# Output weights with the latents' gates folded in, and a context tile with weights of its own

## The chip, the cores and the metric

The kernel runs on one core of a Trainium2 chip. A core has five engines that work side by side, each through its own queue of instructions in order: TensorE (PE, matrix products into PSUM), VectorE (DVE), ScalarE (ACT), GpSimd (POOL) and SyncE (SP), which here issues nearly all DMAs. The metric is the time of one execution in microseconds on the device. Before the change the median of three runs is 2587.82 us (2584.45 to 2589.98).

## The reference

One layer of a hybrid diffusion backbone is computed for 128 context tokens and 2048 latent tokens, all in fp32. Cut to the part that the change touches:

```python
def block(x, s0, mod, ...):
    sh1, sc1, ga1, sh2, sc2, ga2 = mod
    h = rmsnorm(x, norm_mix_l) * (1.0 + sc1) + sh1
    o, s_new = mixer(h, s0, ...)          # ends with: out @ w_out_l
    x = x + ga1 * o
    h = rmsnorm(x, norm_ffn_l) * (1.0 + sc2) + sh2
    x = x + ga2 * (jnp.square(jax.nn.relu(h @ w_ff1_l)) @ w_ff2_l)
    return x, s_new
```

The mixer runs a gated DeltaNet scan forwards and backwards in chunks (four heads of 128) beside a gated spatial MLP (four groups of 128), and projects both together by `w_out` (1024 x 1024). `ga1` is a row of 1024 gates, one for each output column. Context and latent tokens are conditioned by different vectors, so they have different gate rows, and the weights are the same for both. Since `ga1` scales columns of the output, `ga1 * (out @ w_out)` equals `out @ (w_out * ga1)`.

## The kernel before

Tokens are worked on in 17 tiles of 128: tile 0 is the context, tiles 1 to 16 are the latents. The program has a first stage (modulation vectors, input projection, convolution; about 0 to 455 us), a **first scan pass** over the tiles 0 to 16 (forward scan, units 0 to 16), a **second scan pass** (backward scan, units 17 to 33: tile 0, then tiles 16 down to 1), and an MLP stage from about 1235 us on. During the second pass each tile's output is normalised, multiplied by its gate of the mixer, projected by `w_out`, and added to the residual (`o_steps`, line 1317).

**Products in three parts.** Most large products are made by `mm3` (line 238): both operands are split into a high and a low part in fp32r, and three matmuls (high x high, high x low, low x high) are accumulated, at lines 242 to 244. `split_w` (line 194) makes the parts of a weight piece of 128 x 512: the high part by a ScalarE copy, the low part by a DVE subtraction; with a scale (lines 199 and 200) the rows are scaled at the same time. Some products are plain fp32 matmuls of one instruction: the scan's (`quad`, line 1011), the first modulation sums (line 353, two stationary columns) and the row scale of the first stage (line 482).

**The output projection.** `load_wo` (line 1305) loads the sixteen pieces of `w_out` (two column halves n, eight row pieces k) through the stage pool `sp`, which has NS = 4 buffers, and splits them with `wscale`, a scale for each row. It also loads the two halves of the latents' gate row, spread over 128 partitions (`wrow`, line 232). For each tile `trans` (line 1340) transposes the mixer's two halves on TensorE (line 1350) and splits the result into oH (ScalarE, line 1353) and oL (DVE, line 1354). `proj` (line 1359) accumulates two weight pieces a step, eight steps a tile. After the last piece of a half, DVE multiplies the PSUM result by the gate (line 1373, into tmp) and adds tmp to x (line 1374), which is stored to x2_d. Tile 0 loads the context's gate row for this (line 1371).

**What else the second pass does.** For tiles above 8 the steps of `h2_steps` (line 852) prepare the MLP's input in the same pass; their `put` (line 900) splits pieces into opH and opL in the stage buffers and stores them to hop_d. The scan's operands (KK, QK, gb, kt, kT, vt, qT) come back from device memory, and SP issues their loads.

**What sets the order.** Each step is an event with a time in units (`at`, line 1390; `spread`, line 1393): unit i's scan lies at i - 0.51 to i + 1.06 in the first pass, its weights at 16.75 to 18.2, tile 0's `trans` at 18.36 to 18.64 and its `proj` at 18.66 to 19.66. The steps are written in the order of their times, and the framework's planner (line 2015) then orders each queue by its own estimate of when operands and buffers are ready, in favour of what was written first. So a load can be issued far ahead of its use when its buffer is free. "Fill" steps are held behind the scan and its preparation on TensorE by added dependencies (line 1491). Each queue is then strictly in order: an instruction that waits holds all behind it.

Of the kernel before, what the change touches and what calls it, by code (L numbers as in the profile page):

```python
# [8 lines left out]
F32 = mybir.dt.float32  # L9
# [4 lines left out]
ALU = mybir.AluOpType  # L14
# [3 lines left out]
P = 128  # L18
D = 1024
KT = D // P  # L20
# [3 lines left out]
H = 4  # L24
# [41 lines left out]
def hybrid_step(  # L66
# [7 lines left out]
    V, A, G, T = nc.vector, nc.scalar, nc.gpsimd, nc.tensor  # L74
    load = nc.sync.dma_start
    store = nc.sync.dma_start
# [36 lines left out]
    hop_d = {(g, o): dp.tile([P, 4, 2, 4, P], F32, name=f"hop_{g}_{o}_d") for g in range(2) for o in range(1, 8)}  # L113
    z_d = [dp.tile([4 if a else 1, P, 2, NK, P], F32, name=f"z{a}_d") for a in range(5)]
    s1_d, s2_d = ([dp.tile([4, P, NK, P], F32, name=f"s{i}{g}_d") for g in range(2)] for i in (1, 2))
    t_d = {(i, k): dp.tile([P, 512], F32, name=f"t{i}_{k}_d") for i in (5, 6, 7, 4) for k in range(NK)}


# [70 lines left out]
    def raw_w(src, pool=None, tag="w"):  # L189
        t = (pool or wp).tile([P, 512], F32, tag=tag, name="raw")  # L190
        load(out=t, in_=src)
        return t
# [13 lines left out]
    def load_split(src, scale=None):  # L206
        return split_w(raw_w(src, sp, "raw"), scale)
# [24 lines left out]
    def wrow(row):  # L232

        t = w512("row")
        load(out=t, in_=row.to_broadcast([P, 512]))
        return t

    def mm3(ps, trip, first=True, last=True, more=False):

        n = len(trip)  # L240
        for i, (lh, ll, rh, rl) in enumerate(trip):
            T.matmul(ps, lh, rh, start=first and i == 0, stop=False, skip_group_check=more)  # L242
            T.matmul(ps, lh, rl, start=False, stop=False, skip_group_check=more)  # L243
            T.matmul(ps, ll, rh, start=False, stop=last and i == n - 1, skip_group_check=more)  # L244
# [51 lines left out]
    with ExitStack() as ph:  # L296
# [5 lines left out]
        def pj(dt=F32):  # L302
            return ppj.tile([P, 512], dt, tag="pj", name="pj", bufs=3)
# [657 lines left out]
    with ExitStack() as ph:  # L961
# [332 lines left out]
        def fpart(name):  # L1294
            return fp.tile([P, 512], F32, tag="part", name=name, bufs=5)
# [6 lines left out]

        ga1 = []

        def load_wo(n, k):
            if k == 0:
                ga1.append(wrow(mod_d[1:2, 2 * D + n * 512 : 2 * D + n * 512 + 512]))
                WO.append([])
            WO[n].append(load_split(w_out[0, k * P : (k + 1) * P, n * 512 : (n + 1) * 512], wscale[:, k : k + 1]))

        def o_loads(u):
            t = u["t"]
# [4 lines left out]
        def o_steps(du):  # L1317
            t = du["t"]
            out = []
            u = {}  # L1320

            def norm():
                du["ob"] = w512("ob")
                load(out=du["ob"], in_=ob_d[t * P : (t + 1) * P, :])
                o, ga = du["o"], du["ga"]
                ss = smp.tile([P, 4], F32, tag="oss", name="oss")
                junk = fp.tile([P, P], BF16, tag="junk", name="junk", bufs=1)
                for h in range(H):
                    A.activation(junk, o[:, h, :], AF.Square, accum_out=ss[:, h : h + 1])
                r2 = smp.tile([P, 4], F32, tag="r2", name="r2")  # L1330
                rr = smp.tile([P, 4], F32, tag="rr", name="rr")
                V.tensor_tensor(out=r2, in0=rq[:, t, :], in1=rq[:, t, :], op=ALU.mult)
                V.tensor_tensor(out=r2, in0=r2, in1=ss, op=ALU.mult)
                rsqrt_cols(rr, r2, 4, 1.0 / P, EPS)
                V.scalar_tensor_tensor(out=rr, in0=rr, scalar=0.5, in1=rq[:, t, :], op0=ALU.mult, op1=ALU.mult)
                for h in range(H):
                    V.scalar_tensor_tensor(out=o[:, h, :], in0=o[:, h, :], scalar=rr[:, h : h + 1],
                                           in1=ga[:, h * P : (h + 1) * P], op0=ALU.mult, op1=ALU.mult)

            def trans(half):  # L1340
                def f():
                    if half == 0:
                        u["H"], u["L"] = [], []
                        u["x"] = [w512("x"), w512("x")]
                        for n in range(2):
                            load(out=u["x"][n], in_=xrow(t)[:, n * 512 : (n + 1) * 512])
                    src = du["o"] if half == 0 else du["ob"].rearrange("p (h d) -> p h d", h=H)
                    ps = pj().rearrange("p (h d) -> p h d", h=H)
                    for h in range(H):
                        T.transpose(ps[:, h, :], src[:, h, :], ident)  # L1350
                    hs = hp.tile([P, 4, P], F32R, tag="h", name="oH")
                    ls = hp.tile([P, 4, P], F32R, tag="h", name="oL")
                    A.copy(hs, ps)
                    V.tensor_tensor(out=ls, in0=ps, in1=f32(hs), op=ALU.subtract)
                    u["H"] += [hs[:, i, :] for i in range(4)]
                    u["L"] += [ls[:, i, :] for i in range(4)]
                return f

            def proj(n, k0):
                def f():  # L1360
                    if k0 == 0:
                        u["ps"] = pj()
                    for k in (k0, k0 + 1):
                        mm3(u["ps"], [(u["H"][k], u["L"][k]) + WO[n][k]], first=k == 0,
                            last=k == KT - 1)
                    if k0 == KT - 2:
                        sl = slice(n * 512, (n + 1) * 512)
                        tmp = fp.tile([P, 512], F32, tag="ug" if n else "vg", name="tmp")
                        ga = ga1[n]
                        if cond(t) == 0:  # L1370
                            ga = wrow(mod_d[0:1, 2 * D + n * 512 : 2 * D + n * 512 + 512])
                        x = u["x"][n]
                        V.tensor_tensor(out=tmp, in0=u["ps"], in1=ga, op=ALU.mult)
                        V.tensor_tensor(out=x, in0=x, in1=tmp, op=ALU.add)
                        du["x2"] = u["x"]
                        store(out=x2_d[t * P : (t + 1) * P, sl], in_=x)
                return f

            for n in range(2):
                for k0 in range(0, KT, 2):  # L1380
                    out.append(proj(n, k0))
            return [norm, trans(0), trans(1)], out
# [10 lines left out]
        def spread(t0, t1, steps, kind):  # L1393
            for j, st in enumerate(steps):
                at(t0 + (t1 - t0) * (j + 0.5) / len(steps), st, kind)
# [84 lines left out]
        flat = flat[NF:]  # L1480
        spread(p2[4], p2[5], flat, "fill")
        wo = [lambda n=n, k=k: load_wo(n, k) for n in range(2) for k in range(KT)]
        spread(16.75, 17.4, wo[:6], None)
        spread(17.45, 18.2, wo[6:], None)
        tend = max(e[0] for e in events if e[3] == "prep")
# [574 lines left out]
```

## Time and profile before

| | before |
|---|---|
| median of three runs | 2587.82 us (2584.45 to 2589.98) |
| the profiled execution | 2589.03 us |
| its span, first to last instruction | 2587.1 us |
| granted TensorE clock | 0.999 |
| DMA, mean over the span | 221 GB/s |

In the tables of windows each engine has its busy time in that stretch and, in brackets, its number of instructions; after them stand the granted clock, the mean busy share of the 16 DMA engines and the GB/s moved. Matmuls are pipelined: their recorded durations overlap, so the distance between two starts is the cost of one in a row. In the view of one line the three figures are the shortest, the median and the longest duration in ns, then the first and the last start in us. In the chain of waits, which follows the work that ended last back to what released it, each piece has its start, its length and its name; the "by line" row gives each line's share of the stretch.

### The profile page before, as it was taken

Reading aid. Unit: us, or ns where it says so; the run is one execution under the profiler, and the core shown is the slowest. Engines: PE = TensorE matmul, PEld = TensorE weight load, DVE = VectorE, ACT = ScalarE, POOL = GpSimd, SP = SyncE. Lnnn points to the kernel's source line nnn. Section 1 sums busy time; section 2 is a strip of 40 time slices with the busy share of each in tenths; the row PEclk is TensorE's granted clock in tenths of the full one; section 3 lists DMA queues with packets and bytes.
Section 4 is the critical chain, followed back from the end, with each engine's and each line's share of the span. In section 5 each row is a group of like instructions: output and inputs, shape, how many; then the busy total and the mean of one; then the engine's idle time right before and its main releaser. Section 6 shows DMA issues by size and latency. Waiting matters only on the chain.

```text
span 2587.1 us, 44754 instructions
## 1 busy us (share of the span) xinstructions
PE 2547.4 (98%) x15556; PEld 2154.5 (83%) x15556; DVE 1805.3 (70%) x3738; ACT 1221.0 (47%) x3051; POOL 233.7 (9%) x448
## 2 busy tenths in 40 slices
PE   9999999999999999999999999999999999999998
PEld 5899998788888787788888888888888888888887
DVE  5867757766677878886678876666665557784875
ACT  4755556555555667764345543333342432342442
POOL 3112212111111111210000000000000000000000
PEclk9999999999999999999999999999999999999999
DMA  8977737644454656885868788444479979786683
GB/s 287 300 219 213 211 111 253 229 154 155 144 160 151 215 177 235 281 275 183 280 205 252 230 289 293 122 115 118 120 239 368 345 257 327 266 257 204 223 266 112
DMA packets 494695, 571.88 MB, mean 221 GB/s; under 512 B 35124, under 2 KB 297564, under 8 KB 490886
## 3 DMA queue, kind: packets, MB, share of 16 engines
q1 hardware_dynamic: 494470, 569.04, 67.8%
q8 instruction: 122, 2.00, 0.3%
q14 instruction: 103, 0.84, 0.1%
HBM read 389.23 MB, written 179.67 MB: 220 GB/s over the span
## 4 chain that ended last, share of the span: by engine, by line
PE 86%; DMA 6%; DVE 5%; ACT 2%; issue 1%; SPq 0%; POOL 0%; POOLq 0%; DVEq 0%; ACTq 0%
PE f L242 16%; PE f L244 16%; PE f L243 16%; PE pj L242 7%; PE pj L244 6%; PE pj L243 6%; PE pd L1011 4%; PE f L1646 2%; PE pm L242 1%; PE pm L244 1%; PE pm L243 1%; PE pt L626 1%; DMA QK<-qk_d 1%; DMA raw<-in_w_mod_dram 1%; DMA hop_d<-opL 1%
## 5 line engine op out<-in xcount | busy, mean ns | idle before, releaser
L242 PE MATMUL f<-hop,zH 128*128 128x512 f32 (+1 forms) x976 | 376.2, 386 | 1.2 <-ACT zH L1532 1.2
L243 PE MATMUL f<-hop,zH 128*128 128x512 f32 (+1 forms) x976 | 376.1, 386 | 0.0
L244 PE MATMUL f<-hop,zL 128*128 128x512 f32 (+1 forms) x976 | 376.1, 386 | 0.0
L242 PE MATMUL f<-hop,wH 128*128 128x512 f32 x896 | 355.2, 397 | 0.1
L243 PE MATMUL f<-hop,wH 128*128 128x512 f32 x896 | 349.0, 390 | 0.0
L244 PE MATMUL f<-hop,wL 128*128 128x512 f32 x896 | 347.9, 390 | 0.0
L1532 ACT CAST zH<-zraw 128x512 fp32r<-128x512 f32 x240 | 146.4, 620 | 284.6 <-DMA zraw<-s_d 86.9
L242 PEld LDWEIGHTS f<-hop,zH 128*128 128x128 f32 x976 | 183.3, 188 | 38.5 <-ACT zH L1532 1.6
L244 PEld LDWEIGHTS f<-hop,zL 128*128 128x128 f32 x976 | 183.3, 188 | 37.3 <-DVE zL L1526 0.4
L243 PEld LDWEIGHTS f<-hop,zH 128*128 128x128 f32 x976 | 183.3, 188 | 36.9 <-issue 0.2
L1526 DVE TENSOR_TENSOR zL<-zraw,zH 128x512 fp32r<-128x512 f32 x240 | 162.6, 687 | 72.2 <-ACT zH L1532 55.1
L244 PEld LDWEIGHTS f<-hop,wL 128*128 128x128 f32 x896 | 168.2, 188 | 35.3
L242 PEld LDWEIGHTS f<-hop,wH 128*128 128x128 f32 x896 | 168.5, 188 | 32.8 <-issue 0.5
L243 PEld LDWEIGHTS f<-hop,wH 128*128 128x128 f32 x896 | 168.5, 188 | 32.3
L242 PE MATMUL pj<-kH,wH 128*128 128x386 f32 (+2 forms) x568 | 190.5, 338 | 1.3 <-ACT junk L602 1.1
L243 PE MATMUL pj<-kL,wH 128*128 128x386 f32 (+2 forms) x568 | 189.5, 335 | 0.5 <-POOL kL L511 0.5
L244 PE MATMUL pj<-kH,wL 128*128 128x386 f32 (+2 forms) x568 | 189.7, 335 | 0.0
L185 POOL TENSOR_TENSOR r<-rsq,nhalf 128x1 f32<-128x1 f32 (+1 forms) x37 | 25.1, 679 | 1418.0 <-DVE rsq L184 1418.0
L572 DVE SCALAR_TENSOR_TENSOR cv<-pj,vec,cv 128x384 f32<-128x384 f32 (+2 forms) x164 | 87.0, 539 | 52.7 <-ACT cv L569 51.4
L242 PEld LDWEIGHTS pj<-kH,wH 128*128 128x128 f32 x568 | 107.0, 189 | 4.6 <-issue 2.6
L1532 ACT CAST wH<-s 128x512 fp32r<-128x512 f32 x96 | 59.4, 621 | 105.5 <-DVE s L1526 103.5
L243 PEld LDWEIGHTS pj<-kL,wH 128*128 128x128 f32 x568 | 107.4, 189 | 1.4 <-POOL kL L511 0.8
(410 smaller groups left out, 5703.9 us busy)
## 6 DMA issues: line engine op xcount, KB each, us to landing
zraw<-z_d SPq DMA_DIRECT2D x212, 256.0 KB
raw<-in_w_ff_dram SPq DMA_DIRECT2D x128, 256.0 KB
hop<-hop_d SPq DMA_DIRECT2D x28, 1024.0 KB
z_d<-c SPq DMA_DIRECT2D x96, 256.0 KB
zraw<-s_d SPq DMA_DIRECT2D x96, 256.0 KB
raw<-in_w_mod_dram SPq DMA_DIRECT2D x80, 256.0 KB
r<-in_w_ff_dram SPq DMA_DIRECT2D x80, 256.0 KB
s_d<-s SPq DMA_DIRECT2D x64, 256.0 KB
```

The source lines that it names most:

```text
L185: G.tensor_tensor(out=out, in0=t[:np_, :n], in1=nhalf[:np_, :n], op=ALU.pow)
L242: T.matmul(ps, lh, rh, start=first and i == 0, stop=False, skip_group_check=more)
L243: T.matmul(ps, lh, rl, start=False, stop=False, skip_group_check=more)
L244: T.matmul(ps, ll, rh, start=False, stop=last and i == n - 1, skip_group_check=more)
L572: V.scalar_tensor_tensor(out=cv[:, o : o + m], in0=ps[:, s + sh : s + sh + m], scalar=convw[:, w, j : j + 1], in1=cv[:, o : o + m], op0=AL ...
L626: T.matmul(ps[:, i * P : (i + 1) * P], kTt[:, i * P : (i + 1) * P], rhs[:, i * P : (i + 1) * P], start=True, stop=True)
L1011: T.matmul(p[:, h, :], lhs[:, h, :], rhs[:, h, :], start=True, stop=True)
L1526: V.tensor_tensor(out=out, in0=a, in1=b, op=op)
L1532: A.copy(h, src)
L1646: T.matmul(ps[:, c : c + P], self.raw[m, kh][:, kp, :], x0[kh][:, kp, :], start=first and kp == 0, stop=last and kp == 3)
```

## The change

In the first pass, between the event times 2.0 and 15.0, `gate_wo` loads each of the sixteen pieces of `w_out`, multiplies it on DVE by the latents' gate row, and stores it to a new array wo_d in device memory. `load_wo` then loads the pieces from there. So the projection of tiles 1 to 16 already holds the gate: line 1373's multiplication goes for them, and x is added to straight from PSUM. Tile 0 needs other gates, so it takes `w_out` itself, piece by piece through the stage buffers and without a split: its transposed activations are scaled by `wscale` on DVE into one fp32 tile, and each piece is one fp32 matmul in place of `mm3`'s three. It keeps the multiplication by its own gate row.

```diff
+    wo_d = {(n, k): dp.tile([P, 512], F32, name=f"wo{n}_{k}_d") for n in range(2) for k in range(KT)}
...
+        def wo_piece(n, k):
+            return w_out[0, k * P : (k + 1) * P, n * 512 : (n + 1) * 512]
+
+        def gate_wo(n, k):
+
+            if k == 0:
+                ga1.append(fpart("row"))
+                load(out=ga1[n], in_=mod_d[1:2, 2 * D + n * 512 : 2 * D + n * 512 + 512].to_broadcast([P, 512]))
+            raw = raw_w(wo_piece(n, k), sp, "raw")
+            V.tensor_tensor(out=raw, in0=raw, in1=ga1[n], op=ALU.mult)
+            store(out=wo_d[n, k], in_=raw)
+
         def load_wo(n, k):
             if k == 0:
-                ga1.append(wrow(mod_d[1:2, 2 * D + n * 512 : 2 * D + n * 512 + 512]))
                 WO.append([])
-            WO[n].append(load_split(w_out[0, k * P : (k + 1) * P, n * 512 : (n + 1) * 512], wscale[:, k : k + 1]))
+            WO[n].append(load_split(wo_d[n, k], wscale[:, k : k + 1]))
...
+                    if t == 0:
+                        hs = hp.tile([P, 4, P], F32, tag="h", name="o32")
+                        V.tensor_tensor(out=hs, in0=ps, in1=wscale[:, 4 * half : 4 * half + 4].unsqueeze(2)
+                                        .to_broadcast([P, 4, P]), op=ALU.mult)
+                        u["H"] += [hs[:, i, :] for i in range(4)]
+                        if half:
+                            raws(0)
+                        return
...
+            def raws(m):
+
+                for m in range(m, min(m + 2, 2 * KT)):
+                    u["raw", m] = raw_w(wo_piece(*divmod(m, KT)), sp, "raw")
+
             def proj(n, k0):
                 def f():
                     if k0 == 0:
                         u["ps"] = pj()
+                    if t == 0:
+                        raws(n * KT + k0 + 2)
                     for k in (k0, k0 + 1):
-                        mm3(u["ps"], [(u["H"][k], u["L"][k]) + WO[n][k]], first=k == 0,
-                            last=k == KT - 1)
+                        if t == 0:
+                            T.matmul(u["ps"], u["H"][k], u.pop(("raw", n * KT + k)), start=k == 0, stop=k == KT - 1)
+                        else:
+                            mm3(u["ps"], [(u["H"][k], u["L"][k]) + WO[n][k]], first=k == 0, last=k == KT - 1)
                     if k0 == KT - 2:
                         sl = slice(n * 512, (n + 1) * 512)
-                        tmp = fp.tile([P, 512], F32, tag="ug" if n else "vg", name="tmp")
-                        ga = ga1[n]
+                        x, add = u["x"][n], u["ps"]
                         if cond(t) == 0:
-                            ga = wrow(mod_d[0:1, 2 * D + n * 512 : 2 * D + n * 512 + 512])
-                        x = u["x"][n]
-                        V.tensor_tensor(out=tmp, in0=u["ps"], in1=ga, op=ALU.mult)
-                        V.tensor_tensor(out=x, in0=x, in1=tmp, op=ALU.add)
+                            add = fp.tile([P, 512], F32, tag="ug" if n else "vg", name="tmp")
+                            V.tensor_tensor(out=add, in0=u["ps"],
+                                            in1=wrow(mod_d[0:1, 2 * D + n * 512 : 2 * D + n * 512 + 512]), op=ALU.mult)
+                        V.tensor_tensor(out=x, in0=x, in1=add, op=ALU.add)
...
+        spread(2.0, 15.0, [lambda n=n, k=k: gate_wo(n, k) for n in range(2) for k in range(KT)], None)
         spread(16.75, 17.4, wo[:6], None)
```

## The prediction

> **What bounds the kernel now.** I read the page's head first, then the windows by stage, then the chain of waits in two of the stages.
>
> ```profile
> span 2587.1 us, 44754 instructions
> PE 2547.4 (98%) x15556; PEld 2154.5 (83%) x15556; DVE 1805.3 (70%) x3738; ACT 1221.0 (47%) x3051; POOL 233.7 (9%) x448
> ```
>
> TensorE (PE) looks like the bound everywhere, but 98% is an average over stages. The change works in two of them: the first scan pass, and the second pass with its output projection. In these windows the first is 500 to 800 us, the second 880 to 1170.
>
> ```profile
> core 0: us, PE busy (x) PEld busy (x) DVE busy (x) ACT busy (x) POOL busy (x), PEclk, DMA share, GB/s
> 500.00:800.00 300.00, 296.12 (x2590) 249.75 (x2586) 206.64 (x584) 156.72 (x437) 36.33 (x51) 1.00 0.49 154
> 880.00:920.00 40.00, 35.96 (x332) 29.21 (x331) 31.77 (x84) 24.05 (x78) 7.25 (x8) 1.00 0.71 232
> 920.00:965.00 45.00, 45.00 (x403) 37.38 (x402) 36.24 (x93) 28.79 (x94) 7.30 (x9) 1.00 0.40 127
> 965.00:1110.00 145.00, 135.67 (x1208) 111.92 (x1208) 122.97 (x297) 109.50 (x341) 27.61 (x31) 1.00 0.77 259
> 1110.00:1170.00 60.00, 57.90 (x516) 47.80 (x516) 49.19 (x121) 35.21 (x107) 7.92 (x9) 1.00 0.78 265
> ```
>
> In the first pass VectorE (DVE) has room (206.64 of 300 us) and the DMA engines are half idle (0.49). In the second pass TensorE leaves 4.04 us idle at 880 to 920, 9.33 at 965 to 1110 and 2.10 at 1110 to 1170, 15.5 together, and DVE is busy 85% from 965 to 1110. The chains say who ends last: the first line is of 500 to 800, the second of 965 to 1110.
>
> ```profile
> by line: PE pd L1011 21.3%; PE pj L242 13.3%; PE pj L244 12.2%; PE pj L243 12.1%; PE pm L242 6.9%; PE pm L244 6.4%; PE pm L243 6.3%; PE pd L1094 2.9%; PE pm L1277 2.7%; PE pd L1082 2.6%; PE pd L1096 2.5%; DMA S<-in_state_delta_dram 1.5%; DM
> by line: DMA hop_d<-opL 15.5%; DMA h_d<-ev 6.6%; DMA QK<-qk_d 6.1%; issue 5.3%; DVE opL L905 4.9%; PE pd L1011 4.8%; DMA y<-h_d 3.2%; DVE x L1374 3.1%; DVE tmp L1373 2.7%; PE pj L242 2.7%; DVE KK L1050 2.6%; PE pj L244 2.4%; DVE oL L1354 2.
> ```
>
> In the first pass the PE lines shown make 89.2% of the chain. From 965 to 1110 no PE line has 5%: stores (hop_d, h_d), loads and DVE work carry it. So DVE time is nearly free in the first pass and partly paid for in the second.
>
> **The change, part by part.**
>
> **Gate multiplications taken out of the second pass.** For tiles 1 to 16 line 1373 goes, twice a tile, and line 1374 reads PSUM in place of tmp.
>
> ```profile
> L1374 DVE TENSOR_TENSOR x<-x,tmp x34: 678/684/1115, 913.1 to 1248.2; 128x512 f32<-128x512 f32 x34
> L1373 DVE TENSOR_TENSOR tmp<-pj,row x26: 673/683/692, 911.0 to 1247.4; 128x512 f32<-128x512 f32 x26
> ```
>
> The two lines last the same, one reading PSUM and the other not, so the addition stays at 0.68 us. Gone are 32 x 0.683 = 21.9 us of DVE. If each engine keeps its order, the chain shortens at most by what of line 1373 lies on it: 2.7% of 145 us = 3.9, and two pieces ahead of that window:
>
> ```profile
> 951.35 0.60 DVE tmp L1373
> ...
> 961.45 0.68 DVE tmp L1373
> ```
>
> That is 5.2 us, which I take. Ends: 0, if the stores of hop_d end last anyway, and the 15.5 us of idle PE time, if a lighter DVE lets the planner place the chain better. What is late next are those stores and the QK loads.
>
> **Context tile by plain fp32.** Tile 0's 16 products (two halves, eight weight pieces) become one fp32 matmul each in place of three of fp32r.
>
> ```profile
> 897.07 0.47 PE L242 MATMUL pj<-wH,oH 128*128 128x512 f32 x1
> ...
> 910.18 0.40 PE L242 MATMUL pj<-wH,oH 128*128 128x512 f32 x1
> 910.41 0.39 PE L243 MATMUL pj<-wL,oH 128*128 128x512 f32 x1
> ...
> 918.84 0.40 PE L244 MATMUL pj<-wH,oL 128*128 128x512 f32 x1
> 13.03 4.46 PE L353 MATMUL pj<-raw,scond 128*2 128x512 f32 x10
> L353 PE MATMUL pj<-raw,scond x32: 592/592/592, 13.0 to 27.2; 128*2 128x512 f32 x32
> L482 PE MATMUL pt<-diag,ones x10: 377/486/487, 85.6 to 337.1; 128*128 128x384 f32 x8, 128*128 128x256 f32 x2
> ```
>
> The rows of 910 start 0.23 us apart, so the 48 cost 11.0 us. The nearest fp32 rows of this width are line 353's: ten in 4.46 us, (4.46 - 0.592) / 9 = 0.43 each. They have two stationary columns; line 482 has 128 and lasts 486 ns at 384 columns, 106 ns less for 128 columns less, 0.83 ns a column as in 0.43 / 512. So 16 x 0.43 = 6.9 us, 4.1 saved. The Trainium skill, "FP8 and Floating Point Precision", section "TensorE Precision Notes", gives true fp32 four passes through the array; the rows above speak for about two. By that page the 16 would take 16 x 4 x 0.23 = 14.7 us, 3.7 more than now.
>
> How much of the 4.1 counts? The chain around tile 0's projection (897 to 919 us) is this:
>
> ```profile
> 897.00 1.04 DVE ug L1281 x4
> ...
> 898.07 1.99 DMA ob_d<-ug
> ...
> 901.43 6.24 DMA row<-mod_d
> ...
> 907.73 4.48 DMA gb<-g_d
> ...
> 912.25 0.85 DVE X L1056
> ```
>
> Transfers carry 12.7 of these 22 us and DVE most of the rest, so I count a third: -1.4 (ends 0 and -4.1). In the transposes two casts of ScalarE and two subtractions of DVE become two DVE multiplications:
>
> ```profile
> L1354 DVE TENSOR_TENSOR oL<-pm,oH x26: 673/692/693, 898.0 to 1238.1; 128x512 fp32r<-128x512 f32 x26
> L1353 ACT CAST oH<-pm 128x512 fp32r<-128x512 f32 x26 | 15.6, 604 | 11.6 <-PE pm L1350 11.6
> ```
>
> DVE's work is equal, but TensorE now waits for a DVE result in place of a 0.60 us cast, in a queue that is 79% busy: +0.3 (ends 0 and 1.4, two whole operations).
>
> **Tile 0's own weights.** Sixteen loads of 256 KB (4.19 MB) come new, through the four stage buffers, two pieces ahead.
>
> ```profile
> L191 SPq DMA_DIRECT2D raw<-in_w_out_dram x16: 327/328/383, 461.7 to 870.2; - x16
> 848.50 4.63 DMA raw<-in_w_out_dram
> 848.50 2.88 SPq L191 DMA_DIRECT2D raw<-in_w_out_dram x4
> ```
>
> Four can be loaded once the last shared weight piece is split; twelve, six steps, wait until TensorE frees a buffer. A step now lasts (918.84 + 0.40 - 897.07) / 8 = 2.77 us. A pair of buffers cycles in one issue (2.88 / 4 = 0.72), the landing (4.63) and two matmuls (0.86): 6.2 us, with two pairs 3.1 us a step, 0.33 more than now, six times: +2.0. Each us of landing more costs 6 x 0.5 = 3 us; below 4.0 us of landing it is nothing. Behind a held load the SP queue holds KK, QK, gb and the scan's loads, for which DVE waits. Ends: 0 and, at a landing of 7.18 us (the longest piece quoted below), +9.7.
>
> **Weights gated in the first pass.** Added are 16 loads, 16 multiplications of 0.68 us and 16 stores, between events 2 and 15. One event lasts 22.1 us:
>
> ```profile
> L1201 SPq DMA_DIRECT2D of_d<-o x17: 319/382/660, 510.8 to 865.0; - x17
> 987.27 7.18 DMA hop_d<-opL
> ```
>
> (865.0 - 510.8) / 16, so 13 events are 288 us, and 8.4 MB more make 29 GB/s on top of 154. The 10.9 us of DVE go to a stage where at most 10.8% of the chain isn't PE's; half of that share makes +0.6. A store waits on SP for its multiplication and holds the loads behind it; those loads are issued ahead of use. Ends: 0 and +10.9 (all of it bare). The shared pieces are split at 843 to 879 as before, from wo_d, with the same instructions; the two gate rows are loaded earlier. Nothing for both.
>
> **Sum**: -5.2 - 1.4 + 0.3 + 2.0 + 0.6 = -3.7 us. The profiled execution took 2589.03 us (1.93 around its span), so it would be 2585.3. The median of the runs, 2587.82, lies 1.2 below it: forecast 2584. About 0.2% (5.2 us) is what a measurement can tell from no change.
>
> **The rivals.**
>
> *More than the chain shows.* The planner orders every queue anew, and with 1.4 us less DVE work a tile the second pass loses two thirds of its 15.5 us of idle PE time: -10, time 2578. For it: 85% DVE from 965 to 1110. Against: the stores of hop_d on that chain stay.
>
> *DVE's saving is absorbed.* DVE comes earlier to opL and waits for the same landing of hop_d (15.5% of that chain); of the 5.2 only 1 is left: +0.5, time 2588.
>
> *Slower: tile 0's loads.* Place: 898 to 920 us, where DMA is already 71% busy. At 232 / 0.71 = 327 GB/s, 4.19 MB take 12.8 us, more than the 0.29 x 40 = 11.6 us that are free. Landings stretch to 7.18 us, the six steps cost 9.7 in place of 2.0, and the held SP queue brings QK and gb late for two units, some 2 us each: -3.7 + 7.7 + 4 = +8, time 2596. It decides from a landing of 5.9 us on (the sum is then 0). For it: row took 6.24 there. Against: four pieces come early and the planner may load more before 897.
>
> *Four passes.* By the rows this means 0.92 us a matmul, TensorE 3.7 us busier at tile 0; a third counts, +1.2 in place of -1.4: -1.1, time 2587. The page named above has this rule; both fp32 rows are against it.
>
> **How the numbers follow.** Chances: forecast 0.38, more than the chain 0.24, absorbed 0.16, slower by loads 0.18, four passes 0.04. The forecast's own range is 2581 to 2587, and -5.2 lies within it, so it gives 0.16 to faster and 0.22 to same. With the second case faster by over 0.2% is 0.40; the absorbed and four-pass cases lie within 0.2%, about 0.41 in all; slower 0.19. The range reaches from below the second case's 2578 (a full 15.5 would give 2572) to the loads rival: 2574 to 2596.
>
> **What would show it.** Line 1373 twice in all, the additions at 0.68 us from PSUM; DVE in 965 to 1110 down by about 9 us, and PE idle there below 9. Tile 0's 16 fp32 matmuls 0.43 us apart where nothing holds them; 0.9 would be four passes. A wait of PE for raw between 897 and 920 of some 2 us; over 8, or QK late on DVE, is the slower rival. In the first pass 16 multiplications by ga1, and PE idle as now (3.9 of 300). The forecast is wrong if the second pass keeps its length without line 1373, or if the first gets longer by over 2 us.

## The result and the profile after

The kernel with the change takes 2600.8 us (median; the undisturbed runs lie between 2599.07 and 2601.29), the kernel before 2588.97 us (2584.45 to 2590.78) on the same chip. The ratio is 1.0051, with a 95% interval of 1.0039 to 1.0063: slower by half a per cent, about 13 us, where 2584.0 and at most 2596.0 were predicted. One further execution of the new kernel, 2927.53 us at a granted clock of 0.81, is left out of the ratio. The profiled execution took 2600.8 us, 11.8 more than that of before. First the head of its page:

```profile
span 2599.0 us, 44804 instructions
PE 2555.8 (98%) x15540; PEld 2157.4 (83%) x15540; DVE 1792.2 (69%) x3722; ACT 1218.3 (47%) x3049; POOL 232.3 (9%) x448
```

DVE is busy 13.1 us less than before (1805.3), and TensorE 8.4 us more, though it runs 16 instructions fewer. So the work was taken off DVE as planned, and the time did not follow. Where the 11.8 us arise is read from instructions that both kernels have. The views of three tiles of after give them, with the first and the last start at the end of a row: the stores of the scan's output in the first pass (of_d), the stores of the gated weights (wo_d), and a product of the MLP stage (x, raw).

```profile
L1202 SPq DMA_DIRECT2D of_d<-o x17: 319/357/407, 516.8 to 868.8; - x17
...
L1316 SPq DMA_DIRECT2D wo_d<-raw x16: 319/358/1042, 476.2 to 520.7; - x16
...
L1675 PE MATMUL f<-x,raw x512: 269/275/276, 1553.0 to 1915.2; 128*128 128x128 f32 x171
```

Before, the of_d stores went from 510.8 to 865.0, and the MLP product from 1542.1 on, by the same view of before:

```profile
L1646 PE MATMUL f<-x,raw x512: 270/275/275, 1542.1 to 1904.2; 128*128 128x128 f32 x171
```

So unit 0 of the first pass ends 6.0 us late, unit 16 3.8 us late, and the MLP stage begins 10.9 us late. The loss arises in two places: about 6 us before 517 us (of which 2.2 come back), and about 7 between 869 us and the MLP stage. The middle row names the first place. The sixteen gated weights, which were to be spread over 288 us, were all loaded and multiplied, and their stores issued, by 521 us.

The windows of these places, first of before, then of after; in each row the length is followed by the busy time of PE, PEld, DVE, ACT and POOL, then the granted clock, the DMA share and the GB/s:

```profile
480.00:500.00 20.00, 20.00 (x188) 16.23 (x185) 14.62 (x40) 11.56 (x29) 2.93 (x4) 1.00 0.45 143
500.00:520.00 20.00, 18.54 (x173) 15.52 (x169) 13.20 (x39) 10.40 (x30) 2.93 (x4) 1.00 0.60 182
...
900.00:920.00 20.00, 18.72 (x165) 14.75 (x164) 13.02 (x34) 10.83 (x37) 3.31 (x4) 1.00 0.87 277
920.00:940.00 20.00, 20.00 (x185) 16.57 (x185) 15.96 (x40) 12.42 (x42) 3.02 (x4) 1.00 0.42 131
```

```profile
480.00:500.00 20.00, 19.13 (x171) 15.49 (x170) 15.18 (x40) 10.46 (x27) 3.74 (x4) 1.00 0.82 275
500.00:520.00 20.00, 15.67 (x115) 13.07 (x115) 12.43 (x30) 8.21 (x24) 0.00 (x0) 0.83 0.91 299
...
900.00:920.00 20.00, 17.39 (x129) 12.27 (x128) 11.82 (x32) 10.36 (x36) 2.19 (x3) 0.88 0.67 223
920.00:940.00 20.00, 19.40 (x146) 13.47 (x146) 12.22 (x30) 8.46 (x26) 2.02 (x4) 1.00 0.77 278
965.00:1110.00 145.00, 137.25 (x1222) 112.97 (x1222) 113.75 (x287) 107.05 (x331) 26.26 (x30) 1.00 0.74 252
```

At 500 to 520 us the DMA share rose from 0.60 to 0.91, TensorE began 115 instructions in place of 173, and its clock fell to 0.83. At 900 to 920 us the clock is 0.88, and in 900 to 940 TensorE begins 75 instructions fewer. From 965 to 1110 us DVE's work fell by 9.2 us (122.97 before), but TensorE's idle time only by 1.6 (7.75 in place of 9.33).

**The first place.** Unit 1 of the scan starts from the latents' initial state S, which is loaded when unit 0 has ended. The issue of this load on SP's queue and the first TensorE product that reads it, in the timelines of before and then of after; a bracket gives the idle time ahead of a row and what ended it:

```profile
498.93 0.43 SPq L1410 DMA_DIRECT2D S<-in_state_delta_dram  x1
...
503.42 1.13 PE L1011 MATMUL pd<-S,kT 128*128 128x128 f32 x8 [1.46 <-DMA S<-in_state_delta_dram]
```

```profile
500.96 0.43 SPq L1438 DMA_DIRECT2D S<-in_state_delta_dram  x1
501.48 0.45 SPq L1316 DMA_DIRECT2D wo_d<-raw  x1
...
506.97 2.04 PE L1012 MATMUL pd<-S,kT 128*128 128x128 f32 x8 [3.98 <-DMA wo_d<-raw]
508.80 1.91 PE L1012 MATMUL pd<-S,qT 128*128 128x128 f32 x8
510.37 0.77 PE L243 MATMUL pm<-wH,hH 128*128 128x512 f32 x1
510.94 0.63 PE L244 MATMUL pm<-wL,hH 128*128 128x512 f32 x1
...
514.88 1.05 PE L1012 MATMUL pd<-vn,QK 128*128 128x128 f32 x8
```

The load is issued 2.0 us later, and from its issue to the product 6.0 us pass in place of 4.5: TensorE waits 3.98 us in place of 1.46. The profile puts the wait to a store of wo_d, but the operand is S, and in e2_tile0_shared (below) the same wait of 3.8 us is put to the load of S. After the wait TensorE runs slowly: eight products take 2.04 us where a few us later eight of the same size take 1.05, and fp32r products start 0.57 us apart (510.37, 510.94) where the prediction's rows have 0.23; the granted clock is 0.50 from 506 to 512 us and 1.00 again from 514.

**The second place.** The view of line 1392, tile 0's fp32 products, in after:

```profile
L1392 PE MATMUL pj<-raw,o x32: 590/592/908, 904.4 to 938.1; 128*128 128x512 f32 x32
...
  DMA raw<-in_w_out_dram: 7.3, 8
```

Then its waits for raw from 880 to 940 us, of the matmuls (PE) and of the weight loads ahead of them (PEld), in the view of waits (total us, times, longest), and TensorE's timeline:

```profile
PE pj L1392 <- DMA raw<-in_w_out_dram: 3.0, 3, 1.8
PEld pj L1392 <- DMA raw<-in_w_out_dram: 4.3, 5, 2.0
...
899.01 0.40 PE L1095 MATMUL pd<-P,X 128*128 128x64 f16 x4 [1.93 <-DVE P L1087]
...
902.12 2.06 PE L1012 MATMUL pd<-vs,kt 128*128 128x128 f32 x8
...
904.41 3.91 PE L1392 MATMUL pj<-raw,o 128*128 128x512 f32 x8
...
910.95 1.98 PE L1392 MATMUL pj<-raw,o 128*128 128x512 f32 x4 [0.77 <-DMA raw<-in_w_out_dram]
...
919.28 1.98 PE L1392 MATMUL pj<-raw,o 128*128 128x512 f32 x4 [1.84 <-DMA raw<-in_w_out_dram]
...
921.34 1.14 PE L1012 MATMUL pd<-vt,T 128*128 128x128 f32 x8
```

The sixteen products are 32 records: one fp32 product is two. In the row of 910.95 four records start (1.98 - 0.592) / 3 = 0.46 us apart, so a product costs some 0.9 us, and the 16 that were put at 6.9 us take over 14. The loads of raw held TensorE's matmuls three times, 3.0 us in all; the first view's eight times and 7.3 us add to these the waits of the weight loads, most of which are the same gaps seen a second time. The projection lasts from 904.4 to 938.7 us; before it went from 897.07 to 919.24.

The low clock of this place is not due to the waits for raw. It is granted at 0.50 from 900 to 904 us, ahead of tile 0's first product, and eight scan products take 2.06 us there; from 906 us on, across all three waits for raw, it is 1.00, and eight take 1.14. Ahead of this stretch TensorE waits 1.93 us for P of DVE, and DVE's work had come late, because it waited for QK. The same operation on DVE in after and in e5_fp32_resident (below), which has no loads for tile 0:

```profile
891.86 0.69 DVE L1101 TENSOR_TENSOR QK<-QK,E 128x512 f32<-128x512 f32 x1 [1.55 <-DMA QK<-qk_d]
```

```profile
889.93 0.69 DVE L1101 TENSOR_TENSOR QK<-QK,E 128x512 f32<-128x512 f32 x1 [0.32 <-DMA QK<-qk_d]
```

SP issues this load of QK 18.8 us after the last of_d store in both (887.57 and 886.87), so it is not the issue that is late but the landing: DVE begins 4.3 us after the issue in place of 3.1, with four of tile 0's loads issued just before (874 to 885 us). P follows 6.7 us behind this operation in both.

### The profile page after: what moved, and what is told of

Read it like the earlier page. It is cut to its first block, busy times and chain, and to the rows that moved or that the text cites. A ratio compares the mean times of both kernels' runs of the same rounds, so it can differ in the third digit from the quotient of the medians.

```text
span 2599.0 us, 44804 instructions
## 1 busy us (share of the span) xinstructions
PE 2555.8 (98%) x15540; PEld 2157.4 (83%) x15540; DVE 1792.2 (69%) x3722; ACT 1218.3 (47%) x3049; POOL 232.3 (9%) x448
## 5 line engine op out<-in xcount | busy, mean ns | idle before, releaser
L245 PEld LDWEIGHTS pj<-kH,wL 128*128 128x128 f32 x568 | 107.6, 189 | 0.4
```

## The experiments

Twelve kernels, each timed in five rounds beside the kernel before on the same chip. "First pass" gives the first and last start of the seventeen of_d stores, "MLP" the start of the MLP product shown above, both in the profiled execution, whose own time stands last.

| kernel | ratio to before, 95% interval | first pass, us | MLP, us | profiled, us |
|---|---|---|---|---|
| before | 1 | 510.8 to 865.0 | 1542.1 | 2589.03 |
| after | 1.0051 (1.0039 to 1.0063) | 516.8 to 868.8 | 1553.0 | 2600.80 |
| e1_gates_held | 1.0041 (1.0029 to 1.0053) | 510.0 to 865.3 | 1550.7 | 2597.97 |
| e2_tile0_shared | 1.0020 (1.0011 to 1.0028) | 516.8 to 869.5 | 1545.6 | 2592.58 |
| e3_burst_alone | 1.0039 (1.0026 to 1.0052) | 520.7 to 872.8 | 1547.8 | 2597.29 |
| e4_nomul_alone | 1.0006 (0.9997 to 1.0015) | 511.2 to 863.8 | 1542.6 | 2589.47 |
| e5_fp32_resident | 1.0036 (1.0023 to 1.0049) | 516.5 to 868.1 | 1546.2 | 2593.37 |
| e6_held_shared | 1.0015 (1.0006 to 1.0024) | 508.9 to 863.4 | 1539.0 | 2585.76 |
| e7_nomul_six | 0.9988 (0.9978 to 0.9998) | 509.6 to 862.2 | 1538.4 | 2585.51 |
| e8_six | 1.0009 (1.0001 to 1.0018) | 511.1 to 863.9 | 1540.7 | 2587.48 |
| e10_held_alone | 1.0020 (1.0011 to 1.0030) | 511.2 to 868.6 | 1543.2 | 2590.20 |
| e11_ratio | 1.0010 (1.0001 to 1.0019) | 511.2 to 871.4 | 1547.0 | 2594.32 |
| e12_held_nomul | 1.0032 (1.0021 to 1.0042) | 513.3 to 871.5 | 1546.8 | 2595.93 |
| e13_held_nostore | 1.0016 (1.0006 to 1.0025) | 510.6 to 866.0 | 1541.2 | 2588.38 |

0.1% is 2.6 us. Single executions of one kernel differ by several us (e6's profiled one lies 2.8 below its median, e11's 3.6 above), so what a kernel costs is read from the ratios, and where it arises from the traces.

### The three parts: e1, e2, e3 and e4

**e1_gates_held** is after with the sixteen gatings bound to their units: each load waits on SP until its unit's scan loads have been issued.

```diff
-            at(i - 1, lambda i=i, u=u: after_weights(u["scan_loads"], LATER.get(i, ()), (SP,)))
+            at(i - 1, lambda i=i, u=u: noted(("scan", i), lambda: after_weights(u["scan_loads"], LATER.get(i, ()), (SP,))))
...
-        spread(2.0, 15.0, [lambda n=n, k=k: gate_wo(n, k) for n in range(2) for k in range(KT)], None)
+        for j in range(2 * KT):
+            time = 2.0 + 13.0 * (j + 0.5) / (2 * KT)
+            at(time, lambda j=j, i=int(time) + 1: after_weights(lambda: gate_wo(*divmod(j, KT)), (("scan", i),), (SP,)))
```

> The changed kernel with each of the 16 gate multiplications' loads held on SP behind the scan loads of the unit in which the change meant it to be, so that they lie over the whole first pass. Theory: 7.5 of the 11 us that the changed kernel lost arise where all 16 were brought forward to 460 to 521 us, so the time falls from 2600.8 to about 2593, and the first unit's scan runs as before (TensorE idle at 500 to 520 as before, 1.5 us in place of 4.3). Rival 1, the added work itself (10.9 us of DVE, 8.4 MB) costs wherever it lies: 2599 to 2601. Rival 2, the shift at 480 to 520 comes from another order of the planner, not from the gates: 2600.

**e2_tile0_shared** is after with tile 0 on the shared weights, by `mm3`, without loads of its own: `if t == 0` becomes false in `trans` and `proj`, and the calls of `raws` go.

> The changed kernel, but tile 0 is projected by the shared pieces in three fp32r matmuls each, as before, without loads of its own; so tile 0's output has the latents' gates in it as well as its own. The gates' burst at 460 to 521 stays. Theory: tile 0's new way costs 6 us between 895 and 940, so 2595. Rival, it costs only the matmuls: TensorE's records show 32 for tile 0, 0.43 us each, 13.8 us against 11.0, so 2598. Second rival, tile 0 is not the cause and the shift there is what the gates' order carries on: 2600 or 2601.

**e3_burst_alone** is before with `gate_wo` added in the first pass as after has it; nothing reads wo_d.

```diff
+        spread(2.0, 15.0, [lambda n=n, k=k: gate_wo(n, k) for n in range(2) for k in range(KT)], None)
```

> The kernel before with one part of the change added: the 16 pieces are loaded, multiplied by the gates and stored in the first pass as the change writes it, but nobody reads the result (the projection is as before). Theory: the 16 are brought forward into the start of the first pass and cost 7.5 us there: 2596 to 2597. Rival, the loss at that place belongs to the changed order of the rest: 2589 to 2591.

**e4_nomul_alone** is before without line 1373 for tiles 1 to 16, PSUM added directly; the latents' gate rows, which nothing reads then, are not loaded.

```diff
-                        tmp = fp.tile([P, 512], F32, tag="ug" if n else "vg", name="tmp")
-                        ga = ga1[n]
...
-                        x = u["x"][n]
-                        V.tensor_tensor(out=tmp, in0=u["ps"], in1=ga, op=ALU.mult)
+                        x, tmp = u["x"][n], u["ps"]
+                        if cond(t) == 0:
...
                         V.tensor_tensor(out=x, in0=x, in1=tmp, op=ALU.add)
```

> The kernel before with only line 1373 left out for the tiles 1 to 16, so the latents' projection is added without its gates; nothing takes its place. It measures what 21.9 us less DVE in the second pass are worth. My forecast took 5.2 us: 2584. Theory now, from the two traces (the changed kernel gained nothing between 940 and 1235 us): nothing, 2588 to 2590. The third case, more than the chain shows: 2579.

Measured: 1.0041, 1.0020, 1.0039 and 1.0006. Of these e2 is apart from after without overlap of the intervals: tile 0 costs 1.0051 / 1.0020, some 0.3% or 8 us. e4 says that the relief of DVE, the prediction's largest term, is worth nothing that can be measured. e3 says that the gating alone costs 0.39%. The windows of e3 and, below them, of e10_held_alone, the same gating held as in e1:

```profile
480.00:500.00 20.00, 17.68 (x149) 13.82 (x149) 14.61 (x35) 7.69 (x20) 2.29 (x3) 0.91 0.79 264
500.00:520.00 20.00, 14.83 (x115) 12.71 (x112) 11.89 (x34) 7.48 (x21) 1.01 (x1) 0.91 0.92 314
```

```profile
500.00:520.00 20.00, 18.45 (x166) 15.32 (x165) 13.05 (x38) 10.38 (x30) 2.99 (x4) 1.00 0.57 178
```

With the gating held, the stretch is as before (18.54 busy, clock 1.00), and unit 0's store starts at 511.2 in place of 520.7. In the timelines of the same two kernels the load of S is issued 6.8 us later than before in e3, and 0.35 us later in e10:

```profile
505.76 0.43 SPq L1421 DMA_DIRECT2D S<-in_state_delta_dram  x1
...
511.73 0.46 PE L1012 MATMUL pd<-S,kT 128*128 128x128 f32 x2 [3.37 <-issue]
```

```profile
499.28 0.43 SPq L1421 DMA_DIRECT2D S<-in_state_delta_dram  x1
...
503.86 1.13 PE L1012 MATMUL pd<-S,kT 128*128 128x128 f32 x8 [1.55 <-DMA S<-in_state_delta_dram]
```

In e3 unit 0 itself is late, ahead of S. From 474 to 515 us TensorE waits 5.1 us for P of DVE (1.6 in after, 0.4 in e10, and no such wait is listed for before), and P stands on DVE behind gate multiplications, one of which waits for its weights, as the timelines of DVE and then of TensorE in e3 show:

```profile
502.36 0.69 DVE L1313 TENSOR_TENSOR raw<-raw,row 128x512 f32<-128x512 f32 x1 [1.88 <-DMA raw<-in_w_out_dram]
502.97 0.42 DVE L1087 TENSOR_TENSOR P<-pd,sm 128x256 f16<-128x256 f32 x1
...
503.44 0.29 PE L1095 MATMUL pd<-P,X 128*128 128x64 f16 x4 [1.80 <-DVE P L1087]
```

So the bunching and its loss at 480 to 520 us are shown, and the gatings hold the scan in two ways: on DVE, where they stand ahead of P, and through S, which is issued and lands later. But e1, which does away with it, is only 0.10% below after, with intervals that overlap; its marks are 0.3 us late at the end of the first pass and 8.6 at the MLP stage, and between them lies tile 0, whose loads it keeps. The parts don't add up either: 0.39 for the gating, 0.31 for tile 0 and 0.06 for the relief make 0.76, and after has 0.51. A delay in the first pass comes back in part later (e3: 9.9 us at its first store, 7.8 at its last, 5.7 at the MLP stage).

### What at tile 0: e5 and e6

**e5_fp32_resident** is after with tile 0's fp32 products kept and the loads gone.

```diff
-                            T.matmul(u["ps"], u["H"][k], u.pop(("raw", n * KT + k)), start=k == 0, stop=k == KT - 1)
+                            T.matmul(u["ps"], u["H"][k], f32(WO[n][k][0]), start=k == 0, stop=k == KT - 1)
```

> The changed kernel, but tile 0's fp32 matmuls read the shared pieces' high parts, which are in SBUF already, so its 16 loads go; tile 0's output is that of the latents' gated high parts. It parts tile 0's cost, 8 us (ratio to before 1.0051 for the changed kernel, 1.0020 with tile 0 by the shared pieces). Theory, both count: 32 records of 0.43 us against 48 of 0.23 make 2.8 us and the loads the rest, so a ratio of 1.0031. Rival, the matmuls make all of it: 1.005. Second rival, the loads make all of it: 1.002.

**e6_held_shared** is e1 and e2 together.

> The changed kernel with the gate multiplications held over the whole first pass and tile 0 projected by the shared pieces (its output then has both gates): what is left of the change is the gating, well placed, and line 1373's absence. Theory: about 1 us for the gating and nothing gained, a ratio of 1.0005. Rival, the gating costs in the second pass too, through the pieces read back from device memory: what the held gates' run (1.0041) leaves after tile 0's 0.0031, 1.0010 or more. If the absence of line 1373 gains 5 us after all, 0.9985.

e5's 1.0036 lies between after (1.0051) and e2 (1.0020): by the ratios the loads cost 0.15% (4 us) and the fp32 products 0.16% (4 us). Each step by itself is within its intervals; the whole isn't, and it shows again between e1 and e6 (1.0041 and 1.0015). The marks divide it otherwise: from the last of_d store to the MLP stage after loses 7.1 us, e5 1.0, and e2 gains 1.0, which makes 6.1 for the loads and 2.0 for the products. Of the 6.1 only 3.5 arise by 934 us (the scan product pd<-vn,QK starts 64.9 us after the last of_d store in after, 61.4 in e5); the rest comes later, where the cause is not shown. So the loads cost some 4 to 6 us and the products 2 to 4. With tile 0 as before and the gating held, e6 is 1.0015, within the interval of e10 below, which has the held gating alone: the missing line 1373 gains nothing that shows. The number is that of e6's rival (1.0010 or more), but e10, which reads no piece back, accounts for it. In e5 the matmuls run unheld, and the clock stays up, in its timeline of TensorE and its window:

```profile
906.42 1.88 PE L1388 MATMUL pj<-wH,o 128*128 128x512 f32 x4
```

```profile
900.00:920.00 20.00, 19.32 (x132) 11.80 (x132) 12.68 (x35) 9.11 (x32) 4.02 (x4) 1.00 0.72 244
```

Four records start (1.88 - 0.592) / 3 = 0.43 us apart, so a product is 0.86 us with nothing that holds it, and sixteen take 13.8 us where the 48 of fp32r took 11.0: 2.8 more, with TensorE busy for 19.32 of the 20 us. With the loads gone the window's clock is 1.00, against 0.88 in after. e1 keeps the loads and has a stretch at half clock too (0.50 from 896 to 900, after DVE waited 1.66 us for QK). But e2, without loads for tile 0 and with 0.44 us of that wait, still has a shorter one (0.59 and 0.56 from 898 to 902). So the loads go with the longer stretch; that they alone cause it is not shown.

### Why the relief gave nothing: e4, e7 and e8

Two of DVE's waits from 965 to 1110 us, as the view of waits has them for before and for e4 (total us, times, longest):

```profile
DVE opL L905 <- DMA hop_d<-opL: 4.3, 2, 2.4
...
DVE d L910 <- DMA y<-h_d: 1.4, 1, 1.4
```

```profile
DVE opL L905 <- DMA hop_d<-opL: 8.5, 4, 3.2
DVE d L910 <- DMA y<-h_d: 6.2, 3, 3.3
```

and e4's window there:

```profile
965.00:1110.00 145.00, 134.62 (x1186) 110.50 (x1185) 112.97 (x284) 106.54 (x333) 25.88 (x30) 1.00 0.77 257
```

DVE lost 10.0 us of work (122.97 to 112.97) and these two waits grew by 9.0 us (5.7 to 14.7); TensorE's idle time did not fall (9.33 to 10.38). opL is written into one of the stage buffers, and the buffer is free only when its last store to hop_d has landed. If that is the reason, two more buffers for opH and opL should release the gain. **e7_nomul_six** is e4 with opH in the two buffers that tmp had, which leaves the four stage buffers to opL; **e8_six** is the control, before with the same buffers and all multiplications (tmp in place in PSUM).

```diff
         def fhalf(name, dt):
+            if name == "opH":
+                turn.append(0)
+                return fp.tile([P, 512], dt, tag="ug" if len(turn) % 2 else "vg", name=name)
             return sp.tile([P, 512], dt, tag="raw", name=name)
```

> The kernel before without line 1373 for the tiles 1 to 16 (the latents' projection is added without its gates), and with two more buffers for the pieces stored to hop_d: opH goes to the two buffers that tmp had. Theory of the buffers: the 9 us of DVE taken from 965 to 1110 came back as waits of DVE for landings (hop_d 4.3 to 8.5 us, y from h_d 1.4 to 6.2); with six buffers the hop_d part goes, and some 4 us are gained: ratio 0.998 to 0.9985. Rival: the round trip through h_d or the scan's own chain ends next, and nothing is gained: 1.0000 to 1.0006, with DVE's wait for opL gone all the same.

> The control for the run before: the kernel before with every gate multiplication kept (tmp is written in place in PSUM), and opH in the two buffers that this frees. Theory: DVE itself is still as busy as before, so nothing or little is gained, 0.999 to 1.0005. Rival, the buffers alone are the bound: 0.998 or less.

e7 is 0.9988 and e8 1.0009: 0.2% apart, without overlap of the intervals. In e7 the wait for hop_d<-opL is gone; other waits remain, of which those for QK and for opH are longer than in e4:

```profile
DVE QK L1100 <- DMA QK<-qk_d: 7.1, 6, 1.9
...
DVE d L910 <- DMA y<-h_d: 4.3, 2, 2.9
DVE opL L905 <- ACT opH L904: 2.9, 3, 1.0
```

So by the ratios the relief is worth some 0.2% once two buffers more are there, and nothing without them. That it was the buffers which held it is likely but not shown: by the marks e7 gains 2.8 us before 865 us, where nothing but the planner's order differs, and only 0.9 us from there to the MLP stage. The control also keeps a PSUM tile longer, since it writes tmp there, and what that costs was not measured.

### What the gating costs when it is spread: e10, e12 and e13

**e10_held_alone** is e3 with the gating held as in e1.

> The kernel before, plus the 16 gate multiplications and stores in the first pass, whose result nobody reads, but each held on SP behind the scan loads of its unit. With the same work brought forward to the start of the pass the ratio was 1.0039. Theory: what costs is the place, since there the transfers hold up the first unit's scan and the TensorE clock drops; held, the work costs about 1 us: 1.0000 to 1.0010, and the clock at 500 to 520 is 1.00. Rival: 8.4 MB and 10.9 us of DVE cost wherever they are: 1.002 or more.

1.0020: about half of e3's 0.39% is left, where the theory had nearly nothing. The view of wo_d shows that the stores were spread as meant:

```profile
L1314 SPq DMA_DIRECT2D wo_d<-raw x16: 319/320/327, 526.8 to 792.3; - x16
```

**e12_held_nomul** and **e13_held_nostore** are e10 without the sixteen multiplications, and without the sixteen stores.

```diff
-            V.tensor_tensor(out=raw, in0=raw, in1=gr[n], op=ALU.mult)
             store(out=wo_d[n, k], in_=raw)
```

```diff
             V.tensor_tensor(out=raw, in0=raw, in1=gr[n], op=ALU.mult)
-            store(out=wo_d[n, k], in_=raw)
```

> The kernel before with the sixteen held loads and stores of the first pass, but without the sixteen multiplications, so wo_d holds the plain weights; nobody reads wo_d, as in e10_held_alone, and nothing of the outputs is left out. It asks which part of the gating costs the 0.2% that e10 showed when it was spread out. Theory, VectorE's time: sixteen multiplications of 0.69 us are 11 us more work on VectorE, for which TensorE waits most often in this pass (line 1086); without them nothing is left, 0.9995 to 1.0007. Rival, the transfers: 8.4 MB more in the pass and sixteen stores that wait on SP's queue cost it, and it stays at 1.0015 to 1.0030.

> The kernel before with the sixteen held loads and the sixteen multiplications, but without the stores, so the gated weights are thrown away; nothing of the outputs is left out. Theory, VectorE's time: as e10_held_alone, 1.0013 to 1.0030. Rival, the transfers: half of the traffic and all waits of stores on SP are gone, 1.0000 to 1.0010. If neither this nor e12 comes near 1.0020, the cost needs both, or e10's 0.2% was the planner's other order and no one part of the work.

e12 is 1.0032: without DVE's work the cost isn't smaller, so the theory that it is DVE's time falls. e13 is 1.0016, below e12 by the median with intervals that overlap, and within e10's interval: with half of the transfers gone, the cost isn't shown to be smaller. In e12 the loss has the form of the first place, smaller, and at two spots; its windows:

```profile
500.00:520.00 20.00, 17.85 (x144) 15.36 (x144) 11.49 (x31) 8.95 (x26) 1.92 (x3) 0.91 0.49 150
...
800.00:880.00 80.00, 74.48 (x615) 60.70 (x614) 58.03 (x157) 44.98 (x114) 12.66 (x15) 0.96 0.57 182
```

The clock is 0.91 and 0.96, which is 20 x 0.09 + 80 x 0.04 = 5 us of full speed; the first of these lies ahead of the first load of a weight to be gated (524.4), so it is not the gating's own traffic. What the three kernels share are the sixteen loads and an order that the planner made anew. Which of the two costs the 0.2% stays open.

### A version that computes everything: e11

**e11_ratio** puts the mended parts together: gatings held, tile 0 on the shared weights, its PSUM result multiplied by the quotient of the two gate rows (made once in the first pass, and defined only where the latents' gates are not zero), and e7's buffers.

```diff
-                                            in1=wrow(mod_d[0:1, 2 * D + n * 512 : 2 * D + n * 512 + 512]), op=ALU.mult)
+                                            in1=wrow(ratio_d[n : n + 1, :]), op=ALU.mult)
```

> The change with its three dear points mended, computing everything: gates held over the first pass; tile 0 projected by the shared gated pieces in three fp32r matmuls and multiplied by the ratio of the context's to the latents' gates (made once in the first pass) in place of its own gates; opH of h2 in the two buffers that tmp had. Theory: gates held and tile 0 shared gave 1.0015, two more buffers took 0.0018 off where line 1373 was gone: 0.9997, no better than the kernel before. Rival, in the whole version the lighter DVE shows: 0.9985 or less.

1.0010: better than after, with no overlap of the intervals, and still no better than before. What e7 gains (0.12%) is less than what the held gating costs in the first pass (e10, 0.20%), which fits this.

## Why the prediction was wrong, step by step

**Weights gated in the first pass: +0.6 (ends 0 and +10.9).** This step failed most. It priced DVE's work and the mean traffic, both spread "between events 2 and 15". The events' times gave only the order of writing; the planner moved all sixteen to 476 to 521 us, as the section on the kernel says that it can do with loads whose buffers are free. That put DVE's multiplications ahead of the scan's P and made the load of S late. By e3 the step costs 0.39% (0.26 to 0.52), 10 us; spread as assumed it is 0.20% (e10), 5 us in place of 0.6, and not by DVE's time (e12). The sentence "a store waits on SP for its multiplication and holds the loads behind it; those loads are issued ahead of use" named the way, and its second half was wrong for S: this load can't be ahead, because it follows unit 0.

**Context tile by plain fp32: -4.1, of which -1.4 counted.** The sign was wrong. Line 353's records were taken for one matmul each. It has 64 (32 into pj, quoted, and as many into pm), and the code makes 32 matmuls there: two records each, which a count against the code would have shown. Measured are 0.86 us a product and +2.8 us for tile 0, by e5 2 to 4 us of the whole time. The Trainium skill, "FP8 and Floating Point Precision", section "TensorE Precision Notes", gives true fp32 four passes; the trace agrees: 2 x 0.43 = 0.86 us against 4 x 0.23 = 0.92. The four-pass rival, to which the prediction gave the smallest chance, was the case by its cost.

**Tile 0's own weights: +2.0 (to +9.7).** Right in kind, within its ends. TensorE's matmuls waited 3.0 us for raw, of which 2.6 by 920 us, near the "some 2 us" that the prediction named as its sign. The loss of time is 4 to 6 us: the later landing of QK, the longer wait for P behind it and the slower clock (0.88 over 20 us) were not in the sum.

**Gate multiplications taken out: -5.2.** DVE got the 9 us that were predicted (9.2 from 965 to 1110), and PE idle did fall below 9 (7.75); nevertheless e4 puts the worth at +0.06% (-0.03 to +0.15). The step that failed is the reading of line 1373's share of the chain as time gained: TensorE's idle time in e4 is no shorter. The rival "DVE's saving is absorbed" named the place where DVE's waits grew, the landing of hop_d (4.3 to 8.5 us); that this alone took the gain is not shown.

**The sum.** The slower rival ended at 2596 by tile 0 alone. Of its two signs, a wait for raw of over 8 us did not come, and QK late on DVE came once, by 1.3 us (1.55 in place of 0.27 before), through a late landing and not SP's queue. The time passed 2596 because the gating's cost came on top, which the prediction had as an end of its term (+10.9) but in no rival. The text's own condition, "or if the first gets longer by over 2 us", was met at the first of seventeen units.

## What to carry to other kernels

Ask of every added load not only what it moves but what keeps it from being issued at once: where a planner orders the queues, a time that is only written down doesn't hold it, and look where in its way a load can't be early, or an engine's queue makes other work wait behind it. Work taken off an engine that waits for transfers can come back as waits, so look up first what its longest waits are put to. And before a duration is taken from a row with a count, the count is checked against the code.

## What the runs showed of the hardware

**A stall of TensorE can cost more than its length.** After the wait of 3.98 us in after, the two groups of eight scan products take 2.04 and 1.91 us, where the like group at 514.88 takes 1.05; the granted clock is 0.50 from 506 to 512, and from 512.7 us on fp32r products again start 0.31 and 0.24 us apart. The Trainium skill, "TensorE: Matmul & The Clock Gate", section "Part 1: The HAM clock gate (the "warmup" mystery)", says that the clock falls to half after an idle window of about 3.4 us and comes back after a busy one; a wait of 3.98 us followed by a half pace for 5.1 us (506.97 to about 512.1) agrees. Not covered by that sentence are stretches ahead of which no single wait of TensorE was over 2.2 us and the clock still fell: 0.91 in e12 at 500 to 520, after a wait of 2.15 us, and 0.50 in after at 900 to 904, after waits of 1.10, 0.27 and 1.93 us from 894 to 899. A wait of 1.84 us ahead of 919.28 in after, and of 1.46 us at 503.42 in before, left it at 1.00.

**An fp32 product is two records of 0.43 us each**, 0.86 together at 512 columns, against 0.69 for the three of fp32r; plain fp32 is the slower of the two here.
